# One decoder layer on one core: the down projection's sums of weights split in thirds with rooms of their own, a fifth room for raw weights, and transfers in pieces

## The chip, the cores and the metric

The kernel runs on one core of a Trainium2 chip. The metric is device time in microseconds (us) of one execution; lower is better. A core has five engines that run side by side, each taking its own instructions strictly in order: TensorE (PE, matrix products), VectorE (DVE), ScalarE (ACT), GpSimd (POOL) and SyncE (SP). SP, ACT and POOL also start DMA transfers between the chip's main memory and the core's on-chip memory. An instruction that waits for a semaphore holds up all that stand behind it on its engine.

## The reference

```python
h = rmsnorm(x, norm_mix_pre[l])
proj = h @ w_in[l]
...
x = x + rmsnorm(mix @ w_out[l], norm_mix_post[l])
h = rmsnorm(x, norm_mlp_pre[l])
u = jnp.square(jax.nn.relu(h @ w_mlp_up[l]))
x = x + rmsnorm(u @ w_mlp_down[l], norm_mlp_post[l])
```

All is float32: 256 rows of x, model width 2048, MLP width 8192. The part left out is a recurrent branch and a windowed attention, merged by gates. The change concerns the last product, `u @ w_mlp_down` (256 x 8192 by 8192 x 2048), called the down projection here.

## The kernel before

**Products in parts.** Every float32 product is made of three products of rounded parts: a matrix is split into a high part (rounded by ScalarE, `whi`, `thi`) and a low part (the rest, subtracted by VectorE, `wlo`, `tlo`), and TensorE adds high x high, high x low and low x high (`product`, L1171).

**The weight stream.** All weights pass through one `Stream`. A chunk of 128 x 2048 is loaded in two halves of 128 x 1024, numbered through the whole kernel; SP loads a half into one of `WRAW` = 4 raw rooms (`wraw`, L86), ScalarE and VectorE split it (`two_parts`, L104 and L105) into one of `WHALF` = 6 rooms for parts. `half()` hands the next half to the caller and runs ahead: six halves split, four more loaded. A raw room comes free when its low part has been made.

**Stages.** The MLP is done in two groups f of 4096 columns of u. In the up stage of a group, 16 pairs p = 0 to 15 of u are made (`a_pair`), each from four halves, and split for use as left operands (`evacuate`, into `uT[p]`). Then come two down passes (n = 0, 1), each for 1024 columns of the result (`down`). The first up stage starts at half 272 and the four down passes at halves 336, 368, 464 and 496; the pair p of a pass uses halves 2p and 2p+1 of it. In the tables below, halves 356 and 357 are pair 10 of the first pass.

**Seven products for eight.** For the pairs in `SEVEN` (0, 1, 3, 4, 6, 7, 9, 10, 12) the 2 x 2 blocks of the product are formed with seven block products instead of eight, at the price of sums: on the left e (in `evacuate`), on the right three sums of weight blocks T1, T3, T4 of 128 x 512 each (`right_sums`, L61 to L64 on VectorE) which are then split too (`split` in `split_sums`, L150 and L151). Such a step takes 21 matmuls of 512 columns; the other pairs (2, 5, 8, 11, 13, 14, 15) take 24. In the steps of `SUMS_FIRST` (0, 3, 6, 9) the products with T1, T3, T4 come first, in the other SEVEN steps last. The split of a step's sums is put off until the SEVEN step before it has been started (`put_off`).

**Sums made early.** For pairs 4, 7 and 10 of each pass (`SUMMED`) the sums are made long before: `sums_ahead`, a generator that goes on by one step with every half that is used, loads the chunk (`early`, POOL), sums it on VectorE, and stores the sums to main memory (`away`). In the pass they are loaded again as three pieces (`second`, L136).

**Rooms.** A pool of 12 units of 16 KB per partition holds h2T (the normed input), the left operands and the `early` chunks. The scheduler orders each engine's instructions by its own model, so the order is told below from the built program.

Of the kernel before, what the change touches and what calls it, by code (L numbers as in the profile page):

```python
# [18 lines left out]
F32 = mybir.dt.float32  # L19
# [6 lines left out]
P = 128  # L26
D = 2048
S = 256
# [10 lines left out]
SEVEN = (0, 1, 3, 4, 6, 7, 9, 10, 12)  # L39
SUMMED = (4, 7, 10)  # L40
SUMS_FIRST = (0, 3, 6, 9)
APART = (6, 7, 9, 10, 12)
PAIRS = 16


# [8 lines left out]
    return parts  # L54


def right_sums(v, a, b, t):

    l, r = slice(0, 512), slice(512, 1024)
    one, two = t[:, 0:1024], t[:, 1024:1536]  # L60
    v.tensor_tensor(one.rearrange("p (a b) -> p a b", a=2), b[:, l].unsqueeze(1).to_broadcast([P, 2, 512]),  # L61
                    a.rearrange("p (a b) -> p a b", a=2), ALU.add)
    v.tensor_tensor(b[:, l], t[:, l], a[:, r], ALU.add)
    v.tensor_tensor(two, b[:, l], b[:, r], ALU.add)  # L64


class Stream:
# [3 lines left out]
    def __init__(self, nc, pool, chunks, room, sums):  # L71
        self.nc, self.pool, self.chunks, self.room, self.sums = nc, pool, chunks, room, sums
        self.raw, self.parts = {}, {}
        self.loaded = self.split = self.at = FIRST
        self.pin = lambda i: i
        self.high = []
        self.summed, self.put_off, self.last_sums, self.now = {}, [], -1, FIRST
        self.side = []

    def load_to(self, n):  # L80
        while self.loaded < min(n, 2 * len(self.chunks)):
            j = self.loaded
            c = slice(j % 2 * 1024, j % 2 * 1024 + 1024)
            t = self.pool.tile([P, 1024], F32, tag="wraw", bufs=WRAW, name=f"wraw{j}")
            summed = j % 2 and self.summed.get(j // 2)
            self.latest = self.nc.sync.dma_start(t, summed[1] if summed else self.chunks[j // 2][:, c])  # L86
            self.raw[j] = t
            self.loaded += 1
# [35 lines left out]
    def split_sums(self, j):  # L124


        self.load_to(j + 2)
        v = self.nc.vector
        a, b = self.raw.pop(j), self.raw.pop(j + 1)
        summed = self.summed.get(j // 2)  # L130
        if summed:
            pieces = []
            for i in range(3):
                c = slice(i * 512, i * 512 + 512)
                pieces.append((c, self.room("second")))
                self.nc.gpsimd.dma_start(pieces[i][1], summed[0][:, c])  # L136
        else:
            t = self.sums_room("t")
            right_sums(v, a, b, t)
            pieces = [(slice(0, 1536), t)]  # L140
        (ahi, alo), (bhi, blo) = self.two_parts(a, j), self.two_parts(b, j + 1)
        l, r = slice(0, 512), slice(512, 1024)
        parts = {"B11": (ahi[:, l], alo[:, l]), "B22": (ahi[:, r], alo[:, r]), "T2": (bhi[:, l], blo[:, l]),
                 "B21": (bhi[:, r], blo[:, r])}
        self.parts[j] = parts

        def split():
            hi, lo = [self.sums_room(n).bitcast(F32R) for n in ("thi", "tlo")]
            for c, t in pieces:
                self.nc.scalar.copy(hi[:, c], t)  # L150
                v.tensor_tensor(lo[:, c], t, hi[:, c].bitcast(F32), ALU.subtract)  # L151
            for i, name in enumerate(("T1", "T3", "T4")):
                c = slice(i * 512, i * 512 + 512)
                parts[name] = hi[:, c], lo[:, c]

        self.put_off.append((self.last_sums, split))
        self.last_sums = j
        self.settle()
# [44 lines left out]
def layer(tc, x, few, kx_first, kx_rest, pos_row, gains, w_q, w_xy, w_rg, w_g, w_rp, w_ap, w_out,  # L203
# [47 lines left out]
    def flat(t):  # L251
        return t.rearrange("p a b c -> p (a b c)")
# [900 lines left out]
    def evacuate(p, u, dst):  # L1153
        nc.vector.scalar_tensor_tensor(wide(u), wide(u), 0.0, r2.unsqueeze(1).to_broadcast([P, 2, S]), ALU.max,
                                       ALU.mult)
        nc.scalar.activation(u, u, AF.Square)
        if p not in SEVEN:
            nc.scalar.copy(dst[:, :, 0, :], wide(u))
            nc.vector.tensor_tensor(dst[:, :, 1, :], wide(u), dst[:, :, 0, :].bitcast(F32), ALU.subtract)
            return  # L1160

        e = u2("e")
        u4, e4 = [t.rearrange("p (a b) -> p a b", a=4) for t in (u, e)]
        nc.vector.tensor_tensor(e4[:, 0:2], u[:, 0:P].unsqueeze(1).to_broadcast([P, 2, P]), u4[:, 1:3], ALU.subtract)
        nc.vector.tensor_tensor(e4[:, 2], e4[:, 1], u4[:, 1], ALU.subtract)
        nc.vector.tensor_tensor(e4[:, 3], e4[:, 2], u4[:, 3], ALU.add)
        for to, of in ((dst[:, :, 0:3], u4[:, 1:4]), (dst[:, :, 3:7], e4)):
            nc.scalar.copy(to[:, 0], of)
            nc.vector.tensor_tensor(to[:, 1], of, to[:, 0].bitcast(F32), ALU.subtract)

    def product(b, a, w, begun, tail=False, shared=False):  # L1171

        for i, (x, y) in enumerate(((0, 0), (0, 1), (1, 0))):
            mm(b, a[x], w[y], start=not begun and i == 0, stop=tail and i == 2, skip_group_check=shared)  # L1174
# [7 lines left out]
    def down(f, n, uT, held, order, finish, early, between=lambda p: None, behind=lambda: None, closing=False):  # L1182
# [20 lines left out]
        for p in range(PAIRS - held - closing):  # L1203
            if p in SEVEN:
                parts = ws.seven()
                names = list(LEFT)
                if p in SUMS_FIRST:
                    names.sort(key=lambda name: LEFT[name][1] not in ("T1", "T3", "T4"))
                else:
                    names.sort(key=lambda name: LEFT[name][1] in ("T1", "T3", "T4"))  # L1210
                for name in names:
                    i, w = LEFT[name]
                    product(banks[name], (uT[p][:, 0, i], uT[p][:, 1, i]), parts[w], name in begun,
                            p == SEVEN[-1] and (name in ("P1", "P6", "Q5", "N7") or closing and name == PLACE[order[-1]]))
                    begun.add(name)
                if p == SEVEN[-1]:
# [47 lines left out]
    for f in range(2):  # L1264
        uT = {}
        rooms = []
        if f:
            ws.side += [sums_ahead(c, 9, 6, lambda: ws.sums_room("t")) for c in summed[9:]]
        full = []
        for p in range(PAIRS):  # L1270
            u = u2("u")
            if f == 0 and p < 2:
                up_pair(p, wide(u))
            else:
                a_pair(h2T, wide(u), PRIO if p == PAIRS - 1 else 0)
            full.append((p, u))
            if f == 0 and p == R2_AT:
                pump(99)
                spread_r2()
                ctx3.close()  # L1280
                pc = ctx2.enter_context(tc.tile_pool(name="pc", bufs=1))
                ws.room = u2
                ws.sums_room = lambda tag: pc.tile([P, 1536], F32, tag=tag, name=tag)
                ws.side += [sums_ahead(c, 7, 4, lambda: ws.sums_room("t")) for c in summed[6:9]]
            if f == 1 or p >= R2_AT:
                for q, u in full:
                    if q in APART:
                        uT[q] = flat(unit(f"seven{f}{q}"))[:, 0 : 14 * P].rearrange("p (a b c) -> p a b c", a=2, b=7)
                    elif q in SEVEN:
                        uT[q] = pc.tile([P, 2, 7, P], F32R, tag="seven", bufs=len(SEVEN) - len(APART),  # L1290
                                        name=f"seven{f}{q}")
                    elif q == PAIRS - 1:
                        uT[q] = pc.tile([P, 2, 2, S], F32R, tag="plain", name=f"plain{f}")
                    else:
                        i = sum(k not in SEVEN for k in range(q))
                        if i % 2 == 0:
                            rooms.append(unit(f"uT{f}{i}"))
                        uT[q] = rooms[i // 2][:, 2 * (i % 2) : 2 * (i % 2) + 2]
# [158 lines left out]
```

## Time and profile before

| | |
|---|---|
| median of 3 runs | 1507.63 us (1503.21 to 1509.97) |
| the profiled execution's own time | 1507.84 us |
| its span in the trace | 1506.1 us |
| TensorE busy | 1485.7 us (99%) |
| VectorE busy | 1132.3 us (75%) |
| ScalarE busy | 843.6 us (56%) |
| GpSimd busy | 40.5 us (3%) |
| main memory read and written | 222 GB/s over the span |

All times in the trace are counted from the span's start. In a row of the timeline stand start, duration, engine, line, operation, out<-in, and in brackets the engine's idle time just before and what ended it. In a row of the groups stand the count, the busy time, the mean duration in ns, and the idle time with what ended it. In the chain of waits stand start, duration and what the end of the run was waiting for then. A line of the page is a line of the kernel above.

### The profile page before, as it was taken

To read this page: it belongs to the slowest core of one execution; us is meant where nothing else is said; L and a number is where in the kernel's file an instruction comes from. 1 tells how busy PE (TensorE), PEld (TensorE's weight loads), DVE (VectorE), ACT (ScalarE), POOL (GpSimd) and SP (SyncE) were. 2 spreads that over 40 slices of the span, in tenths; PEclk is the share of its full clock that TensorE was granted. 3 is DMA by queue.
4 is the path that set the end of the run, shared out by engine and by line. 5 is a ranking of instruction groups with operands and counts; after the bars stand their busy time and mean duration, and the time that the engine had idled before them with its cause. 6 is when DMAs were issued, how large, how long until landed. Compare 5 with 4: busy or idle time off the path is not lost.

```text
span 1506.1 us, 20243 instructions
## 1 busy us (share of the span) xinstructions
PE 1485.7 (99%) x7562; PEld 1254.8 (83%) x7562; DVE 1132.3 (75%) x1439; ACT 843.6 (56%) x1181; POOL 40.5 (3%) x81
## 2 busy tenths in 40 slices
PE   9999999999999999999999999999999999999997
PEld 8887778888889888888889888887778888887776
DVE  6676668759578866666658887787887767689987
ACT  7564565647477674444346655565464555456563
POOL 0000000000000000000000000000000000000000
PEclk9999999999999999999999999999999999999999
DMA  9753544555645659787766676576678666677675
GB/s 338 234 165 134 185 160 139 176 183 188 203 158 193 219 174 343 263 303 249 266 214 234 234 282 224 196 241 219 221 258 301 224 219 227 208 261 240 212 248 189
DMA packets 91971, 336.06 MB, mean 223 GB/s; under 512 B 10465, under 2 KB 10721, under 8 KB 89313
## 3 DMA queue, kind: packets, MB, share of 16 engines
q1 hardware_dynamic: 80352, 288.89, 57.1%
q0 software_dynamic: 8064, 37.75, 6.9%
q10 hardware_dynamic: 3456, 8.13, 1.4%
q8 instruction: 59, 0.97, 0.3%
q14 instruction: 40, 0.32, 0.1%
HBM read 312.71 MB, written 22.02 MB: 222 GB/s over the span
## 4 chain that ended last, share of the span: by engine, by line
PE 74%; DVE 9%; DMA 9%; ACT 4%; issue 3%; DVEq 0%; ACTq 0%; SPq 0%
PE ps L293 21%; PE ps L291 11%; DMA wraw<-in_w_dn 6%; DVE wlo L105 4%; PE pp L335 3%; PE pp L333 3%; PE pp L331 3%; PE g L331 3%; PE g L335 3%; PE g L333 3%; ACT whi L104 2%; PE q L331 2%; PE q L335 2%; PE q L333 2%; PE o L331 2%
## 5 line engine op out<-in xcount | busy, mean ns | idle before, releaser
L104 ACT CAST whi<-wraw 128x1024 fp32r<-128x1024 f32 x516 | 537.4, 1051 | 520.5 <-PE ps L293 103.0
L105 DVE TENSOR_TENSOR wlo<-wraw,whi 128x1024 fp32r<-128x1024 f32 x516 | 623.5, 1220 | 270.4 <-ACT whi L104 266.0
L293 PE MATMUL ps<-h2T,whi 128*128 128x512 f32 x960 | 223.9, 390 | 0.0
L293 PEld LDWEIGHTS ps<-h2T,whi 128*128 128x128 f32 x960 | 178.2, 188 | 35.6
L291 PEld LDWEIGHTS ps<-h2T,wlo 128*128 128x128 f32 x960 | 119.1, 192 | 2.3
L293 PE MATMUL ps<-hT,whi 128*128 128x512 f32 x512 | 120.6, 391 | 0.0
L291 PE MATMUL ps<-h2T,wlo 128*128 128x256 f32 x960 | 119.9, 283 | 0.0
L293 PEld LDWEIGHTS ps<-hT,whi 128*128 128x128 f32 x512 | 94.7, 188 | 19.5 <-issue 0.7
L331 PE MATMUL g<-whi,hT 128*128 128x512 f32 x256 | 101.1, 395 | 0.0
L335 PE MATMUL g<-whi,hT 128*128 128x512 f32 x256 | 99.8, 390 | 0.0
L333 PE MATMUL g<-wlo,hT 128*128 128x512 f32 x256 | 99.7, 390 | 0.0
L1174 PE MATMUL dQ<-whi,uT 128*128 128x512 f32 (+1 forms) x192 | 71.9, 387 | 0.0
L291 PEld LDWEIGHTS ps<-hT,wlo 128*128 128x128 f32 x512 | 63.7, 191 | 2.1 <-issue 0.8
L291 PE MATMUL ps<-hT,wlo 128*128 128x256 f32 x512 | 64.6, 283 | 0.0
L331 PEld LDWEIGHTS g<-whi,hT 128*128 128x128 f32 x256 | 48.1, 188 | 10.5 <-issue 1.0
L335 PEld LDWEIGHTS g<-whi,hT 128*128 128x128 f32 x256 | 48.1, 188 | 10.3
L333 PEld LDWEIGHTS g<-wlo,hT 128*128 128x128 f32 x256 | 48.1, 188 | 9.5
L1174 PE MATMUL s<-whi,seven 128*128 128x512 f32 x144 | 53.5, 389 | 0.0
L331 PE MATMUL q<-whi,hT 128*128 128x512 f32 x128 | 51.1, 400 | 0.0
L1174 PE MATMUL s<-thi,seven 128*128 128x512 f32 x144 | 51.0, 395 | 0.0
L331 PE MATMUL pp<-whi,yrnn 128*128 128x512 f32 x128 | 50.0, 391 | 0.0
L335 PE MATMUL q<-whi,hT 128*128 128x512 f32 x128 | 49.9, 390 | 0.0
(324 smaller groups left out, 2607.5 us busy)
## 6 DMA issues: line engine op xcount, KB each, us to landing
wraw<-in_w_up SPq DMA_DIRECT2D x128, 512.0 KB, 4.4
wraw<-in_w_dn SPq DMA_DIRECT2D x116, 512.0 KB, 4.5
wraw<-in_w_g SPq DMA_DIRECT2D x64, 512.0 KB, 4.4
wraw<-in_w_xy SPq DMA_DIRECT2D x64, 512.0 KB, 4.0
wraw<-in_w_q SPq DMA_DIRECT2D x32, 512.0 KB, 3.7
wraw<-in_w_ap SPq DMA_DIRECT2D x32, 512.0 KB, 3.8
wraw<-in_w_rp SPq DMA_DIRECT2D x32, 512.0 KB, 5.0
wraw<-in_w_out SPq DMA_DIRECT2D x32, 512.0 KB, 4.6
```

The lines of the kernel that those rows point to most:

```text
L104: self.pin(self.nc.scalar.copy(hi, src))
L105: self.pin(self.nc.vector.tensor_tensor(lo, src, hi.bitcast(F32), ALU.subtract))
L291: mm(ps[:, f, 1, :], w, a[:, 0, :], start=False, stop=j == 1 and k == 7)
L293: mm(ps[:, f].rearrange("p a b -> p (a b)"), w, a.rearrange("p a b -> p (a b)"), start=kt == 0, stop=j == 3 and k == 7)
L331: mm(banks[tb][n], a[:, 0, t], hi[:, n * 512 : n * 512 + 512], start=first, stop=False)
L333: mm(banks[tb][n], a[:, 0, t], lo[:, n * 512 : n * 512 + 512], start=False, stop=False)
L335: mm(banks[tb][n], a[:, 1, t], hi[:, n * 512 : n * 512 + 512], start=False, stop=last)
L1174: mm(b, a[x], w[y], start=not begun and i == 0, stop=tail and i == 2, skip_group_check=shared)
```

## The change

The changed kernel does the following:

- **Thirds.** T1, T3 and T4 of a step get a room each for high and low part (`thi` and `tlo`, three rooms of 128 x 512 each, in place of one room each of 128 x 1536). Sums made in the pass are split by three instructions of 512 columns on ScalarE and on VectorE where one of 1536 stood. The sums themselves lie in two rooms (`t1024`, `t512`).
- **Order of products.** In a SEVEN step the products with sums go T1, T3, T4; before, it was T4, T1, T3.
- **A fifth raw room.** From the first up stage on, each half whose number divides by five goes to `xraw`, and the stream loads one half further ahead.
- **Transfers in pieces.** `sums_ahead` loads its chunk in four quarters of 128 x 512, with generator steps between them, and stores sums as 128 x 1024 and 128 x 512, again with steps between. A chunk takes 11 or 16 steps where it took 9, 11 or 15.
- **Left operands.** Two neighbouring pairs share a unit (8 units for 16 pairs); of a SEVEN pair, three of seven blocks lie in a room `three` of their own.

```diff
+    def left(three_four, i):
+        t, k = three_four[i > 2], i if i < 3 else i - 3
+        return t[:, 0, k], t[:, 1, k]
...
+            self.wide = self.wide or self.more and j % (WRAW + 1) == 0
+            t = self.more() if self.wide and j % (WRAW + 1) == 0 else self.pool.tile([P, 1024], F32, tag="wraw", bufs=WRAW, name=f"wraw{j}")
...
-            t = self.sums_room("t")
-            right_sums(v, a, b, t)
-            pieces = [(slice(0, 1536), t)]
+            one, two = self.sums_rooms()
+            right_sums(v, a, b, one, two)
+            pieces = [one[:, 0:512], one[:, 512:1024], two]
...
-            hi, lo = [self.sums_room(n).bitcast(F32R) for n in ("thi", "tlo")]
-            for c, t in pieces:
-                self.nc.scalar.copy(hi[:, c], t)
-                v.tensor_tensor(lo[:, c], t, hi[:, c].bitcast(F32), ALU.subtract)
...
+            for name, t in zip(("T1", "T3", "T4"), pieces):
+                hi, lo = [self.sums_room(n) for n in ("thi", "tlo")]
+                self.nc.scalar.copy(hi, t)
+                v.tensor_tensor(lo, t, hi.bitcast(F32), ALU.subtract)
+                parts[name] = hi, lo
...
-        self.load_to(max(FIRST, j + WHALF) + WRAW)
+        self.load_to(max(FIRST, j + WHALF) + WRAW + bool(self.wide))
...
-    def sums_ahead(c, first, second, room):
+    def sums_ahead(c, gaps, rooms):
         w = flat(unit("early", F32))
-        nc.gpsimd.dma_start(w, chunks[c])
-        for _ in range(first):
+        for i in range(4):
+            nc.gpsimd.dma_start(w[:, quarter(i)], chunks[c][:, quarter(i)])
+            for _ in range(gaps[0]):
+                yield
+        for _ in range(gaps[1]):
             yield
-        t = room()
-        right_sums(nc.vector, w[:, 0:1024], w[:, 1024:2048], t)
-        nc.gpsimd.dma_start(ws.summed[c][0], t)
-        nc.gpsimd.dma_start(ws.summed[c][1], w[:, 1024:2048])
-        for _ in range(second):
-            yield
+        one, two = rooms()
+        right_sums(nc.vector, w[:, 0:1024], w[:, 1024:2048], one, two)
+        to, b = ws.summed[c]
+        for away, of in ((to[:, 0:1024], one), (to[:, 1024:1536], two), (b, w[:, 1024:2048])):
+            nc.gpsimd.dma_start(away, of)
+            for _ in range(gaps[2]):
+                yield
...
-    ws.side += [sums_ahead(c, 5, 4, lambda: flat(unit("early_t", F32))[:, 0:1536]) for c in summed[:6]]
+    ws.side += [sums_ahead(c, (1, 4, 1), unit_rooms) for c in summed[:6]]
...
-            ws.side += [sums_ahead(c, 9, 6, lambda: ws.sums_room("t")) for c in summed[9:]]
+            ws.side += [sums_ahead(c, (2, 5, 1), ws.sums_rooms) for c in summed[9:]]
...
-                ws.sums_room = lambda tag: pc.tile([P, 1536], F32, tag=tag, name=tag)
-                ws.side += [sums_ahead(c, 7, 4, lambda: ws.sums_room("t")) for c in summed[6:9]]
+                ws.more = lambda: pc.tile([P, 1024], F32, tag="xraw", name="xraw")
+                ws.sums_room = lambda tag: pc.tile([P, 512], F32R, tag=tag, bufs=3, name=tag)
+                ws.sums_rooms = lambda: [pc.tile([P, n], F32, tag=f"t{n}", name=f"t{n}") for n in (1024, 512)]
+                ws.side += [sums_ahead(c, (2, 5, 1), ws.sums_rooms) for c in summed[6:9]]
```

What this does to the built order is shown at three places. On VectorE in the first down pass, from the low part of half 357 on, stood before (`t` with `wraw360`, `wraw361`: the sums of pair 12; `tlo` from `t`: pair 9; `tlo` from `second`: pair 10):

```order
L105 TENSOR_TENSOR wlo357_9031<-wraw357_8948,whi357_9030 128x1024
L151 TENSOR_TENSOR tlo_9017<-t_8979,thi_9016 128x1536
L105 TENSOR_TENSOR wlo358_9051<-wraw358_8991,whi358_9050 128x1024
L61 TENSOR_TENSOR t_9103<-wraw361_9036,wraw360_9034 128x1024
L105 TENSOR_TENSOR wlo359_9069<-wraw359_8993,whi359_9068 128x1024
L63 TENSOR_TENSOR wraw361_9036<-t_9103,wraw360_9034 128x512
L151 TENSOR_TENSOR tlo_9096<-second_9020,thi_9095 128x512
L151 TENSOR_TENSOR tlo_9096<-second_9022,thi_9095 128x512
L151 TENSOR_TENSOR tlo_9096<-second_9024,thi_9095 128x512
```

And in the changed kernel stands there:

```order
L105 TENSOR_TENSOR wlo357_9129<-wraw357_9015,whi357_9128 128x1024
L149 TENSOR_TENSOR tlo_9107<-t1024_9068,thi_9106 128x512
L149 TENSOR_TENSOR tlo_9111<-t1024_9068,thi_9110 128x512
L149 TENSOR_TENSOR tlo_9115<-t512_9069,thi_9114 128x512
L59 TENSOR_TENSOR t1024_9205<-wraw361_9132,xraw_9083 128x1024
L105 TENSOR_TENSOR wlo358_9149<-wraw358_9033,whi358_9148 128x1024
L61 TENSOR_TENSOR wraw361_9132<-t1024_9205,xraw_9083 128x512
L62 TENSOR_TENSOR t512_9206<-wraw361_9132 128x512
L105 TENSOR_TENSOR wlo359_9167<-wraw359_9081,whi359_9166 128x1024
L149 TENSOR_TENSOR tlo_9194<-second_9118,thi_9193 128x512
L149 TENSOR_TENSOR tlo_9198<-second_9119,thi_9197 128x512
L149 TENSOR_TENSOR tlo_9202<-second_9120,thi_9201 128x512
```

The first sum of pair 12 moved ahead of the low part of half 358, the last sum ahead of half 359, and pair 9's split became three instructions. Of the 24 places where sums are made in the passes, one had a lower half's low part behind the sums before; now 11 have one or two (pairs 0 and 1 of the first and third pass; pairs 9 and 12 of the first; 0, 9 and 12 of the second; 0 and 12 of the fourth).

On TensorE at the first SEVEN step of the first pass stood (`dQ_8698` is the bank of T4's product, `s_8695` holds those of T1 and T3):

```order
L1174 MATMUL dQ_8698<-thi,seven_7331 128x512
L1174 MATMUL dQ_8698<-tlo,seven_7331 128x512
L1174 MATMUL dQ_8698<-thi,seven_7331 128x512
L1174 MATMUL s_8695<-thi,seven_7331 128x512
L1174 MATMUL s_8695<-tlo,seven_7331 128x512
L1174 MATMUL s_8695<-thi,seven_7331 128x512 x2
```

And now:

```order
L1178 MATMUL s_8750<-thi,uT_7355 128x512
L1178 MATMUL s_8750<-tlo,uT_7355 128x512
L1178 MATMUL s_8750<-thi,uT_7355 128x512 x2
L1178 MATMUL s_8750<-tlo,uT_7355 128x512
L1178 MATMUL s_8750<-thi,uT_7355 128x512
L1178 MATMUL dQ_8753<-thi,three_7356 128x512
```

T4, which is summed last, moved behind T1 and T3.

On POOL's queue in the second down pass (`second<-away_77`: sums of pair 7; `away_79`: of pair 10; `early`: a chunk for the fourth pass) stood:

```order
L136 DMA second<-away_75 128x512 x3
L136 DMA second<-away_77 128x512 x3
L136 DMA second<-away_79 128x512
L361 DMA early<-in_w_dn 128x2048
L136 DMA second<-away_79 128x512 x2
```

And now:

```order
L134 DMA second<-away_75 128x512 x3
L134 DMA second<-away_77 128x512
L358 DMA early<-in_w_dn 128x512 x4
L134 DMA second<-away_77 128x512 x2
L134 DMA second<-away_79 128x512 x3
```

The chunk's load became four, and moved ahead of two of pair 7's pieces. By the program, its unit comes free after pair 1 of that pass; before, it was that of pairs 2 and 5, after pair 5.

More of the change, by code (lines that the diff above doesn't have):

```diff
@@ L78, in __init__ @@
         self.side = []
+        self.more, self.wide = None, False
     def load_to(self, n):
@@ L131, in split_sums @@
         if summed:
[L132 to L136, printed above, removed]
-        else:
-            t = self.sums_room("t")
-            right_sums(v, a, b, t)
-            pieces = [(slice(0, 1536), t)]
+            pieces = [self.room("second") for _ in range(3)]
+            for i, t in enumerate(pieces):
+                self.nc.gpsimd.dma_start(t, summed[0][:, i * 512 : i * 512 + 512])
+        else:
+            one, two = self.sums_rooms()
+            right_sums(v, a, b, one, two)
+            pieces = [one[:, 0:512], one[:, 512:1024], two]
         (ahi, alo), (bhi, blo) = self.two_parts(a, j), self.two_parts(b, j + 1)
@@ L1166, in evacuate @@
         nc.vector.tensor_tensor(e4[:, 3], e4[:, 2], u4[:, 3], ALU.add)
[L1167 removed]
+        for to, of in zip(dst, (u4[:, 1:4], e4)):
             nc.scalar.copy(to[:, 0], of)
@@ L1282, in layer @@
                 ws.room = u2
-                ws.sums_room = lambda tag: pc.tile([P, 1536], F32, tag=tag, name=tag)
-                ws.side += [sums_ahead(c, 7, 4, lambda: ws.sums_room("t")) for c in summed[6:9]]
+                ws.more = lambda: pc.tile([P, 1024], F32, tag="xraw", name="xraw")
+                ws.sums_room = lambda tag: pc.tile([P, 512], F32R, tag=tag, bufs=3, name=tag)
+                ws.sums_rooms = lambda: [pc.tile([P, n], F32, tag=f"t{n}", name=f"t{n}") for n in (1024, 512)]
+                ws.side += [sums_ahead(c, (2, 5, 1), ws.sums_rooms) for c in summed[6:9]]
             if f == 1 or p >= R2_AT:
                 for q, u in full:
[L1287 to L1293, printed above, removed]
-                    else:
[L1295 to L1298, printed above, removed]
+                    if q % 2 == 0:
+                        rooms.append(unit(f"uT{f}{q}"))
+                    room = rooms[-1][:, 2 * (q % 2) : 2 * (q % 2) + 2]
+                    if q in SEVEN:
+                        three = pc.tile([P, 2, 3, P], F32R, tag="three", bufs=len(SEVEN), name=f"three{f}{q}")
+                        uT[q] = three, flat(room).rearrange("p (a b c) -> p a b c", a=2, b=4)
+                    else:
+                        uT[q] = room
                     evacuate(q, u, uT[q])
```

21 lines of the change are left out of this document (8 added, 13 removed).

## The prediction

> **What bounds the kernel now.** I read the page's busy times first, then the windows by stage, then who waited on TensorE.
>
> ```profile
> PE 1485.7 (99%) x7562; PEld 1254.8 (83%) x7562; DVE 1132.3 (75%) x1439; ACT 843.6 (56%) x1181; POOL 40.5 (3%) x81
> 980.00:1066.00 86.00, 83.92 (x362) 68.50 (x361) 72.24 (x74) 46.48 (x50) 3.76 (x7) 0.98 0.68 217
> 1066.00:1152.00 86.00, 81.97 (x357) 66.45 (x356) 67.99 (x70) 44.51 (x48) 6.45 (x12) 1.00 0.81 275
> 1152.00:1323.00 171.00, 171.00 (x982) 151.27 (x981) 124.97 (x154) 94.31 (x117) 3.76 (x7) 1.00 0.67 222
> PE dQ L1174 <- DVE tlo L151: 7.6, 8, 2.1
> PE dQ L1174 <- ACT thi L150: 1.8, 3, 0.9
> ```
>
> TensorE is the bound. In the second up stage (1152 to 1323) it is busy for 171.00 of 171 us: nothing is to be gained there. In the first two down passes it is not (83.92 and 81.97 of 86), and its only long waits are for the split sums, `tlo` and `thi`: 9.4 us in 11 places. That is the part that the change works on.
>
> How much is lost in all comes from start to start, since an end of a matmul is modelled. Rows of the timeline and of the chain of waits:
>
> ```profile
> 980.35 0.39 PE L1174 MATMUL dQ<-thi,seven 128*128 128x512 f32 x1
> 1141.38 2.72 PE dQ L1174 x12
> 1152.26 3.85 PE ps L293 x17
> 1329.91 0.39 PE L1174 MATMUL dQ<-thi,seven 128*128 128x512 f32 x1
> 1493.38 0.28 PE L1174 MATMUL dQ<-whi,uT 128*128 128x256 f32 x1
> 979.00:1153.00 174.00, 165.80 (x714) 134.74 (x714) 0.99 0.74 246
> ```
>
> Twelve matmuls in a row take 2.72 us, 0.2267 each. The first two passes hold 714 (last row): 161.9 us, but last from 980.35 to 1152.26, 171.9 us. **Lost: 10.0 us.** Passes three and four hold 696 of 512 columns up to 1493.38 (714 less the 18 that the kernel makes in halves there): 157.8 us in 163.5. **Lost: 5.7 us.** Together 15.7 us: the most that this change can bring, 1.0% of the time.
>
> The longest loss shows how it comes about. Pair 10 of the first pass, TensorE and then VectorE:
>
> ```profile
> 1033.15 0.39 PE L1174 MATMUL dQ<-thi,seven 128*128 128x512 f32 x1
> 1035.62 0.50 PE L1174 MATMUL dQ<-tlo,seven 128*128 128x512 f32 x1 [2.08 <-DVE tlo L151]
> 1038.51 0.63 PE L1174 MATMUL dQ<-whi,uT 128*128 128x512 f32 x1
> 1016.30 1.89 DVE L151 TENSOR_TENSOR tlo<-second,thi 128x512 fp32r<-128x512 f32 x3
> 1020.44 3.49 DVE L105 TENSOR_TENSOR wlo<-wraw,whi 128x1024 fp32r<-128x1024 f32 x3
> 1023.85 1.75 DVE L151 TENSOR_TENSOR tlo<-t,thi 128x1536 fp32r<-128x1536 f32 x1
> 1025.52 1.22 DVE L105 TENSOR_TENSOR wlo<-wraw,whi 128x1024 fp32r<-128x1024 f32 x1
> 1030.80 1.23 DVE L61 TENSOR_TENSOR t<-wraw,wraw 128x1024 f32<-128x1024 f32 x1 [4.07 <-DMA wraw<-in_w_dn]
> 1033.08 0.68 DVE L63 TENSOR_TENSOR wraw<-t,wraw 128x512 f32<-128x512 f32 x1
> 1033.68 1.89 DVE L151 TENSOR_TENSOR tlo<-second,thi 128x512 fp32r<-128x512 f32 x3
> 1023.96 6.72 DMA wraw<-in_w_dn
> ```
>
> The last `wlo` of the row at 1020.44 (half 357) frees a raw room at 1023.9. The load of half 361 starts into it at 1023.96 and takes 6.72 us. VectorE stands idle for 4.07 us at the sums of pair 12, which need that half; pair 10's `tlo`, whose pieces were ready, stand behind and come at 1033.68. TensorE needs T4, the last piece, at once, and starts at 1035.62. Afterwards its matmuls ran at a lower pace (0.63 long at 1038.51) for about 3 us, which adds some 1.6 us to the 2.2 of the wait.
>
> In the second pass it is pair 3, whose sums are made in the pass:
>
> ```profile
> 1066.25 7.67 DMA wraw<-in_w_dn
> 1076.27 1.24 DVE t L61
> 1079.25 1.48 ACT thi L150
> 1080.77 1.76 DVE L151 TENSOR_TENSOR tlo<-t,thi 128x1536 fp32r<-128x1536 f32 x1 [0.16 <-ACT thi L150]
> 1082.58 0.50 PE L1174 MATMUL dQ<-tlo,seven 128*128 128x512 f32 x1 [1.29 <-DVE tlo L151]
> ```
>
> A load waited for a room, took 7.67 us, then came the sums, one split of 1.48 us, and one of 1.76 us, and only then TensorE. SP's queue of loads in these passes is held by rooms nearly all the time (138 of 172 us):
>
> ```profile
> SPq L86 <- DVE wlo L105: 107.8, 57, 7.2
> SPq L86 <- DVE wraw L63: 30.6, 5, 7.6
> DVE t L61 <- DMA wraw<-in_w_dn: 12.5, 7, 4.1
> ```
>
> **The change part by part.**
>
> *Thirds.* Their cost, from the groups by form:
>
> ```profile
> L151 DVE TENSOR_TENSOR tlo<-t,thi 128x1536 fp32r<-128x1536 f32 x24 | 42.1, 1755 | 2.5 <-ACT thi L150 2.3
> L150 ACT CAST thi<-t 128x1536 fp32r<-128x1536 f32 x24 | 35.4, 1476 | 2.5 <-PE s L1174 1.9 <-DVE t L64 0.6
> L151 DVE TENSOR_TENSOR tlo<-second,thi 128x512 fp32r<-128x512 f32 x36 | 22.6, 684 | 0.0
> L150 ACT CAST thi<-second 128x512 fp32r<-128x512 f32 x36 | 19.9, 616 | 2.9 <-PE s L1174 2.9
> ```
>
> 24 times one instruction becomes three. On VectorE three in a row took 1.89 us (row at 1016.30) against 1.755: 24 x 0.135 = 3.2 us; apart, 3 x 0.684 - 1.755 = 0.297, in all 7.1 us. On ScalarE at most 24 x 0.372 = 8.9 us. I take 3.2, since the order has most of them in a row. VectorE works 72.24 and 67.99 of 86 us in a pass, so 0.8 to 1.8 us a pass fit into its idle time; if that cover were gone, 3.2 to 7.1 us would lie on the path. [...]
>
> What thirds bring: for sums made in the pass, the first product needs 0.62 + 0.68 = 1.30 us of splitting in place of 1.48 + 1.76 = 3.24, 1.9 us sooner; each further third takes 0.68, as long as its three matmuls. For loaded sums, with T1 first, one of three pieces is needed in place of three: 1.89 - 0.68 = 1.2 us sooner. And each third's room comes free for the next step while TensorE still uses the others.
>
> *Fifth room.* A load starts at the low part of the half before: at least one `wlo` sooner (3.49 / 3 = 1.16 us), at most one half of TensorE's work (161.9 us over 64 halves, 2.5 us). Traffic stays the same.
>
> *Order on VectorE.* The scheduler spent part of that room: 11 places have sums ahead of lower halves. At pair 10's place `tlo` now stands behind one more sum of 512 columns, about 0.6 us by the spacing of rows 1033.08 and 1033.68; half 358 stands behind the wait for 361. Per loss, then: sooner by 1.2 + 1.2 - 0.6 = 1.8 us at least and 1.9 + 2.5 = 4.4 at most.
>
> *Pieces.* Twelve chunks, each 3 loads and 1 store more: 48 issues on POOL. From the DMA issues of the first passes and the groups:
>
> ```profile
> early<-in_w_dn POOLq DMA_DIRECT2D x2, 1024.0 KB, 9.0
> second<-away POOLq DMA_DIRECT2D x15, 256.0 KB, 6.2
> L136 POOL DMA_DIRECT2D second<-away x36 | 19.4, 539 | 359.9 <-DVE tlo L151 106.9 <-DVE seven L1169 87.8 <-ACT t L1343 47.0
> ```
>
> 48 x 0.54 = 26 us on an engine that is busy 3%: no cost. The last quarter is loaded 5 or 7 halves before its sum; at 2.72 us a half that is 13.6 or 19 us, over the 9.0 of the whole chunk. Without that cover, VectorE would wait up to 9.0 us in each of twelve places. On POOL's queue in the second pass, the load that now stands ahead of pair 7's pieces waits for pair 1; pair 7's sums are used 28 us later (two plain steps at 5.44, three SEVEN at 4.76, and 12 matmuls), over 9.0 + 6.2. I cost this at nothing. Left operands: the same instructions, at nothing.
>
> *Sum.* The credit of 1.8 to 4.4 us covers most of the 11 waits (the longest idle 2.1 us), but the largest only in part at its lower end, and in the third pass loads of other things share the DMA engines. I leave 4.4 of the 15.7 us: 11.3 recovered, 1507.84 - 11.3 = **1496.5 us**. The profiled execution lies 0.2 us from the median of the runs shown, so the forecast holds for either. Its own range: 1492.1 (all recovered) to 1500.
>
> **The rivals.**
>
> *The order spends the room.* VectorE waits for half 361 as before, only one instruction earlier. For it: the 11 places. Against: the load starts sooner there too. Then only the thirds count, 1.2 us less 0.6 in each of 11 places: 6.6 us, and the time is 1501. Chance 0.16.
>
> *VectorE becomes the bound.* If the idle time in the passes turns out to be no cover, the split costs 3.2 to 7.1 us and the losses stay: 1511 to 1515. Against: 14 and 18 us idle a pass. [...] Chance 0.06.
>
> *The fifth load brings nothing.* If DMA engines limit the loads (share 0.81, 275 GB/s in the second pass), a fifth in flight makes each slower, and it goes as in the first rival or to 1506. Against: 0.68 and 217 GB/s in the first pass, which loses as much. [...] Chance 0.06.
>
> *Slower: near halves stand behind far loads.* In seven places inside the passes (pairs 9 and 12; 0, 9, 12; 0, 12) the low part of a half that TensorE uses earlier waits for a load that it does not need. If VectorE has no lead there, each costs the wait of 4.07 us and a `wlo` of 1.16: 7 x 5.2 = 37 us, 1533 with the gain taken off, 1515 if it is half. It decides from (7.5 + 11.3) / 7 = 2.7 us a place. Against: in the trace half 358 was split by 1026.7 (row at 1025.52) and used at 1038.51, a lead of 12 us. Chance 0.12.
>
> **How the numbers follow.** The forecast has 0.60, the rivals 0.16, 0.06, 0.06 and 0.12. About 0.5%, 7.5 us, is what a measurement of this kernel can tell from no change. Faster by over that (under about 1500) is the forecast: 0.60. Within it lie the first three rivals: 0.28. Slower: 0.12. The range from 1491.5 to 1507 takes in forecast, first rival and part of the third.
>
> **What would show it.** Right: TensorE's waits for `tlo` and `thi` from 9.4 us to under 4, the sums' wait for loads (12.5 us) smaller, first two passes under 167 us, up stages still at 171 of 171. Wrong: waits of TensorE for `wlo`, or new ones before 980 us; SP's wait for rooms unchanged; matmuls longer than 0.39 in more places.

## The result, and the profile after

The changed kernel takes 1497.45 us (median of 6 runs, 1496.26 to 1499.64) where the kernel before took 1505.54 us beside it (6 runs). The ratio is 0.9946, with a 95% interval of 0.9928 to 0.9963: faster by 0.54% (0.37 to 0.72), about the half per cent that can be told from no change. The forecast was 1496.5 us. The profiled execution has a span of 1494.5 us against 1506.1 before, 11.6 us less, and it is this difference that is taken apart below. It is larger than the 8.1 us between the medians, since the profiled execution before took 1507.84 us, 2.3 over its median, and that of the changed kernel 1496.26, 1.2 under its own; these 3.5 us are spread from execution to execution and are not explained here.

The changed kernel's busy times and its windows of the first two down passes and the second up stage; after the duration come busy time and count for TensorE, its weight loads, VectorE, ScalarE and GpSimd, then granted clock, DMA share and GB/s:

```profile
PE 1481.0 (99%) x7562; PEld 1255.3 (84%) x7562; DVE 1133.2 (76%) x1487; ACT 850.9 (57%) x1229; POOL 66.7 (4%) x129
980.00:1066.00 86.00, 86.00 (x387) 71.47 (x386) 76.38 (x91) 51.21 (x67) 4.41 (x9) 1.00 0.70 232
1066.00:1152.00 86.00, 86.00 (x386) 71.43 (x385) 73.16 (x85) 49.91 (x62) 10.14 (x19) 1.00 0.83 289
1152.00:1323.00 171.00, 171.00 (x991) 151.64 (x990) 125.95 (x158) 92.65 (x118) 6.69 (x13) 1.00 0.65 217
```

TensorE is now busy for all of the down passes' windows. From the first to the last matmul of the first two passes, and of passes three and four (timeline of the changed kernel):

```profile
984.88 0.39 PE L1178 MATMUL s<-thi,uT 128*128 128x512 f32 x1
1146.50 0.39 PE L1178 MATMUL dCs<-whi,uT 128*128 128x512 f32 x1
1324.54 0.39 PE L1178 MATMUL s<-thi,uT 128*128 128x512 f32 x1
1486.49 0.28 PE L1178 MATMUL s<-whi,uT 128*128 128x256 f32 x1
```

The first row gives the start of the first of 714 matmuls and the second that of the last, so 161.62 us hold 713 steps of 0.2267: nothing is lost. Measured so in every trace, the kernel before has 171.5 and 167.7 us, the changed one 161.6 and 161.95. So 15.6 of the 15.7 us that the prediction named have gone, where it had expected 11.3.

But the first pass begins at 984.88 us, 4.5 us later than before. All waits of TensorE of over 0.5 us in the changed kernel, with total, times and longest:

```profile
PE o L329 <- DVE wlo L105: 2.9, 1, 2.9
PE warm L433 <- DVE ones L417: 1.1, 1, 1.1
PE kv L455 <- ACT hT L439: 0.8, 1, 0.8
PE o L327 <- ACT whi L104: 0.7, 1, 0.7
```

No wait for `tlo` or `thi` is left. A new one has come, for `wlo` in the projection of the mixer's output (L327 and L329, "o"). TensorE, VectorE and POOL there (the timeline, one engine after the other; in a POOL row L358 is the load of a quarter, L367 a store of sums):

```profile
743.04 0.39 PE L331 MATMUL o<-whi,mixT 128*128 128x512 f32 x1
744.14 0.49 PE L327 MATMUL o<-whi,mixT 128*128 128x512 f32 x1 [0.71 <-ACT whi L104]
747.53 0.50 PE L329 MATMUL o<-wlo,mixT 128*128 128x512 f32 x1 [2.90 <-DVE wlo L105]
752.68 0.40 PE L327 MATMUL o<-whi,mixT 128*128 128x512 f32 x1
...
726.58 4.90 DVE L954 TENSOR_TENSOR xg<-x,g 128x512 f32<-128x512 f32 x8
731.39 1.22 DVE L59 TENSOR_TENSOR early_t<-early 128x1024 f32<-128x1024 f32 x1
745.11 1.23 DVE L59 TENSOR_TENSOR early_t<-early 128x1024 f32<-128x1024 f32 x1 [2.95 <-DMA early<-in_w_dn]
746.26 2.35 DVE L105 TENSOR_TENSOR wlo<-wraw,whi 128x1024 fp32r<-128x1024 f32 x2
...
703.32 1.09 POOL L358 DMA_DIRECT2D early<-in_w_dn  x2 [44.90 <-PE pp L331]
733.02 0.54 POOL L367 DMA_DIRECT2D away<-early_t  x1 [28.62 <-DVE early_t L59]
736.50 0.54 POOL L367 DMA_DIRECT2D away<-early_t  x1 [1.19 <-DVE early_t L62]
737.07 1.11 POOL L358 DMA_DIRECT2D early<-in_w_dn  x2
```

Read from below. POOL issues two quarters of the sixth chunk at 703. Next in its queue stand the three stores of the fifth chunk, and POOL waits 28.62 us for the sums that they carry, which VectorE begins at 731.39, after its work for the norm. Only at 737.07 do the last two quarters of the sixth chunk go. VectorE comes to the sums of that chunk and waits 2.95 us for its third quarter, and the low parts that TensorE needs stand behind. From 743.04 to 752.68 there are 16 steps from matmul to matmul, 3.6 us at 0.2267 each; they took 9.6. So 6.0 us are lost there. The bill of the span: 15.6 us less in the down passes, 6.0 more here, 1.5 less elsewhere before them, 0.5 less at the end: 11.6.

### The profile page after: what moved, and what is told of

Read it like the earlier page. It is cut to its first block, busy times and chain, and to the rows that moved or that the text cites. A ratio compares the mean times of both kernels' runs of the same rounds, so it can differ in the third digit from the quotient of the medians.

```text
span 1494.5 us, 20497 instructions
## 1 busy us (share of the span) xinstructions
PE 1481.0 (99%) x7562; PEld 1255.3 (84%) x7562; DVE 1133.2 (76%) x1487; ACT 850.9 (57%) x1229; POOL 66.7 (4%) x129
## 4 chain that ended last, share of the span: by engine, by line
PE 95%; DVE 2%; DMA 2%; ACT 1%; issue 0%; DVEq 0%; SPq 0%; ACTq 0%
PE ps L289 21%; PE ps L287 11%; PE dQ L1178 8%; PE s L1178 7%; PE dP L1178 4%; PE g L327 4%; PE g L331 4%; PE g L329 4%; PE pp L331 4%; PE pp L327 4%; PE pp L329 4%; PE dCs L1178 3%; PE q L327 2%; PE q L331 2%; PE q L329 2%; PE kv L455 1%
## 5 line engine op out<-in xcount | busy, mean ns | idle before, releaser
L105 DVE TENSOR_TENSOR wlo<-wraw,whi 128x1024 fp32r<-128x1024 f32 x469 | 567.8, 1221 | 245.9 <-ACT whi L104 242.5
L104 ACT CAST whi<-wraw 128x1024 fp32r<-128x1024 f32 x469 | 490.4, 1051 | 439.2 <-PE ps L289 94.2
L1178 PE MATMUL dQ<-whi,uT 128*128 128x512 f32 (+1 forms) x296 | 108.7, 385 | 0.0
L327 PE MATMUL g<-whi,hT 128*128 128x512 f32 x256 | 101.1, 395 | 0.0
L329 PE MATMUL g<-wlo,hT 128*128 128x512 f32 x256 | 99.7, 390 | 0.0
L104 ACT CAST whi<-xraw 128x1024 fp32r<-128x1024 f32 x47 | 49.4, 1052 | 45.6 <-PE ps L289 21.9
L105 DVE TENSOR_TENSOR wlo<-xraw,whi 128x1024 fp32r<-128x1024 f32 x47 | 57.4, 1221 | 14.9 <-ACT whi L104 14.9
L1178 PEld LDWEIGHTS dQ<-whi,uT 128*128 128x128 f32 x296 | 55.2, 188 | 11.2
L148 ACT CAST thi<-t 128x512 fp32r<-128x512 f32 x72 | 41.6, 617 | 31.2 <-PE s L1178 20.0
L327 PEld LDWEIGHTS g<-whi,hT 128*128 128x128 f32 x256 | 48.1, 188 | 10.6 <-issue 1.0
L1178 PE MATMUL dQ<-wlo,uT 128*128 128x512 f32 (+1 forms) x148 | 56.9, 385 | 0.0
L358 POOL DMA_DIRECT2D early<-in_w_dn x48 | 26.1, 543 | 690.1 <-DVE px L317 497.6
```

The costliest lines, as they stand in the source:

```text
L104: self.pin(self.nc.scalar.copy(hi, src))
L105: self.pin(self.nc.vector.tensor_tensor(lo, src, hi.bitcast(F32), ALU.subtract))
L148: self.nc.scalar.copy(hi, t)
L327: mm(banks[tb][n], a[:, 0, t], hi[:, n * 512 : n * 512 + 512], start=first, stop=False)
L329: mm(banks[tb][n], a[:, 0, t], lo[:, n * 512 : n * 512 + 512], start=False, stop=False)
L358: nc.gpsimd.dma_start(w[:, quarter(i)], chunks[c][:, quarter(i)])
```

## The experiments

Two questions were open: whether the loss near 743 us comes from the quarters themselves or from where they stand, and which part of the change filled the down passes. "Lost" is the time of the four down passes, measured as above, over the 323.56 us of the changed kernel. Every ratio is to the kernel before, run beside it; its medians were 1505.5 to 1505.9 us.

**The wait near 743 us.** First run: whole chunks, with the 9, 11 and 15 steps of before (the diff shows the load alone).

```diff
-        for i in range(4):
-            nc.gpsimd.dma_start(w[:, quarter(i)], chunks[c][:, quarter(i)])
...
+        nc.gpsimd.dma_start(w, chunks[c])
```

> The changed kernel with each chunk that is summed ahead loaded in one transfer again, sums 5, 7 or 9 halves later and the three stores in a row, as before the change. Theory (quarters spaced out made the sixth chunk's sums late, and they hold up wlo in the o-projection; in the down passes the quarters do nothing): TensorE's waits for wlo and whi near 743 us (3.6 us, and some 1.5 us of slower matmuls behind them) go, the four down passes stay without a gap, so 1492 to 1493.5 us against 1497.5 of the changed kernel. Rival (whole chunks of 1 MB crowd the loads of the down passes, so the quarters are what filled them): up to 15.7 us of gaps come back there, 1497 to 1505 us.

1493.37 us, ratio 0.9921 (0.9902 to 0.9940). The wait for `wlo` has gone, and 1.0 us is lost in the down passes. So the quarters did not fill those: the rival falls. Since the steps changed with the quarters, this run doesn't tell which of them made the wait.

Second run: the quarters stay, and a chunk takes 7 steps in place of 11.

```diff
-    ws.side += [sums_ahead(c, (1, 4, 1), unit_rooms) for c in summed[:6]]
+    ws.side += [sums_ahead(c, (1, 3, 0), unit_rooms) for c in summed[:6]]
```

> The changed kernel with gaps of (1, 3, 0) in place of (1, 4, 1) for the first six chunks: quarters as in the changed kernel, but 7 halves from chunk to chunk in place of 11, and the three stores in a row. All six are then summed ahead of the o-projection's loads on VectorE. Theory (only the lateness of the sixth chunk costs): the waits near 743 us go, 1492 to 1493.5 us. Rival 1 (the quarters' issues or their spread themselves disturb the stage before 980 us): a wait of some 3 to 5 us remains somewhere between 570 and 980 us, 1496 to 1498 us. Rival 2 (the cover of 3 + 1 halves is too short): VectorE waits for early at several of six places and TensorE with it, over 1498 us.

1492.52 us, ratio 0.9919 (0.9901 to 0.9937); 0.4 us lost in the down passes. Quarters as such cost nothing: what cost was that the sixth chunk came late. To separate this from chance, the changed kernel, this one and one with 8 steps were run together.

> The changed kernel itself once more, on the same chip as the three beside it, so that the 4.6 us at 743 us are read off in the same runs. Theory: 1496 to 1498.5 us, some 4 to 5 us over the run with gaps of (1, 3, 0), with TensorE's wait for wlo at 743 us in its trace. Rival (that wait was chance of one profile): no such wait, and the same time as with (1, 3, 0).

> Gaps of (1, 3, 0) for the first six chunks once more, on the same chip as the changed kernel. Theory: 1491.5 to 1493.5 us. Rival: within 1 us of the changed kernel.

```diff
-    ws.side += [sums_ahead(c, (1, 4, 1), unit_rooms) for c in summed[:6]]
+    ws.side += [sums_ahead(c, (1, 4, 0), unit_rooms) for c in summed[:6]]
```

> Gaps of (1, 4, 0): 8 halves from chunk to chunk, six chunks still summed ahead of the o-projection's loads. Theory (any spacing that has the sixth chunk done by then is as good, the last quarter's cover does not matter): within 1 us of the run with (1, 3, 0). Rival (a longer cover takes away the wait of 1.3 us at 602 us): 1.3 us less.

The changed kernel: 1497.44 us, 0.9946 (0.9933 to 0.9958). Gaps of (1, 3, 0): 1492.24 us, 0.9916 (0.9903 to 0.9930). Gaps of (1, 4, 0): 1492.86 us, 0.9922 (0.9908 to 0.9936). The first two intervals lie apart: 5.2 us. TensorE's longest wait after the first 10 us in the trace of the changed kernel, and in that of (1, 3, 0):

```profile
PE o L329 <- DVE wlo L105: 2.8, 1, 2.8
```

```profile
PE ptr L893 <- DVE g L911: 0.8, 1, 0.8
```

The wait at 743 us is there in each readable trace with 11 steps a chunk, and in none with 7, 8 or 9; the wait for `g`, near 602 us, has gone with 8 as well, but that doesn't show in the medians. Gaps of (1, 3, 0) give a version that beats both kernels; those of (1, 4, 0) are as good within the intervals, so one step of cover more or less makes no difference that can be measured. Gaps of (1, 4, 0) leave out only the steps between the stores of the changed kernel, three for each chunk, and in its trace the wait is gone: these steps brought it.

**The down passes.** Each of the two kinds of rooms was taken away alone, first from the changed kernel.

```diff
-                ws.more = lambda: pc.tile([P, 1024], F32, tag="xraw", name="xraw")
```

> The changed kernel without the fifth room for raw halves: four rooms and one load less in flight, all else as changed. Theory (loads start too late for lack of a room, thirds alone win only 1.2 to 1.9 us less 0.6 in each of 11 places): 5 to 9 of the 15.7 us come back in the down passes, 1502 to 1507 us. Rival (thirds alone do it: splitting and freeing by thirds was what held the sums): the down passes stay without gaps, 1497 to 1498 us.

1499.17 us, 0.9959 (0.9945 to 0.9972). Neither theory's number: only 2.6 us are lost in the down passes, where 5 to 9 had been expected. The rest is the same loss near 743 us.

```diff
-                ws.sums_room = lambda tag: pc.tile([P, 512], F32R, tag=tag, bufs=3, name=tag)
+                ws.sums_room = lambda tag: pc.tile([P, 1536], F32R, tag=tag, name=tag)
...
-            for name, t in zip(("T1", "T3", "T4"), pieces):
-                hi, lo = [self.sums_room(n) for n in ("thi", "tlo")]
+            hi, lo = [self.sums_room(n) for n in ("thi", "tlo")]
+            for c, t in pieces:
```

> The changed kernel with one room of 1536 columns each for the sums and their high and low parts again (sums made in the pass split by one instruction of 1536 columns, and the next split waits until all three products have used the room); fifth room, order of products and quarters as changed. VectorE's work falls by 3 to 7 us in all. Theory (thirds and fifth room each bring a part): 3 to 8 us come back in the down passes, mostly where sums are made in the pass (pair 3 of the second), 1500 to 1505 us. Rival (the fifth room alone does it): no gaps, 1497 to 1498 us, or less with VectorE's work.

1500.30 us, 0.9958 (0.9944 to 0.9972). In the range of the theory, but the loss near 743 us is in it as well, so this alone does not tell the two apart. Its one trace spans 3018 us, twice the others, and says nothing of the waits.

So the four corners were run without that loss, with gaps of (1, 3, 0). Edits as in the two diffs, alone and together:

> The kernel with gaps of (1, 3, 0) for the first six chunks (1492.5 us, no gap in the down passes), with one room of 1536 columns each for sums, high and low parts again: fifth room and new order alone. Without the fifth room but with thirds, the trace showed only 1.3 us of gaps in the down passes. Theory (the two overlap: each alone makes TensorE's operands early enough by about 2 us, so either covers most places): 2 to 4 us of gaps, 1494 to 1497 us. Rival (thirds carry it, the fifth room little): 7 us or more, over 1499 us.

> Gaps of (1, 3, 0), thirds as changed, no fifth room: the fourth corner beside both (1492.5), fifth room alone (1494.6) and neither (1503.75). Theory (the two overlap; without the fifth room the down passes lost 1.1 + 1.4 us in the earlier trace): 1494 to 1496 us. Rival (without the fifth room it loses more once the wait at 743 us is gone, since loads then start elsewhere): over 1497 us.

> The kernel with gaps of (1, 3, 0), with neither the fifth room nor thirds: what is left of the change is the order of products (T1, T3, T4), the rooms of the left operands, and the quarters. Theory (thirds and fifth room overlap, and without both the losses are back, save about 1.2 us at each of the places where loaded sums are used first): 7 to 13 us of gaps in the down passes, 1500 to 1505 us. Rival (the order of products is what did it, and the two rooms are not needed): under 3 us of gaps, 1493 to 1496 us.

| with gaps of (1, 3, 0) | median, us | ratio (95% interval) | lost in the down passes |
|---|---|---|---|
| neither | 1503.75 | 0.9991 (0.9981 to 1.0000) | 10.0 us |
| fifth room alone | 1494.64 | 0.9924 (0.9912 to 0.9937) | 1.3 us |
| thirds alone | 1495.77 | 0.9936 (0.9924 to 0.9949) | 3.1 us |
| both, two sets of runs | 1492.24, 1492.52 | 0.9916, 0.9919 | 0.8 us, 0.4 us |

The theory holds in the times, though the fifth room alone lost 1.3 us where 2 to 4 had been expected: alone the fifth room is worth 9.1 us and thirds 8.0, together 11.2 to 11.5. Not all of these ran side by side; by the ratios it is 10.1, 8.3 and 10.8 to 11.3. They overlap. That both are faster than one alone is not shown by the times, whose intervals overlap; the losses in the traces say so (0.4 and 0.8 us against 1.3 and 3.1). How they overlap is seen at pair 3 of the second pass, where the prediction had seen the sums come too late. In each fence the first sum of the pair, the split of the first third (of the whole in the first two), and TensorE's first product that needs it; neither, fifth room alone, thirds alone, and the changed kernel with both:

```profile
1073.67 1.23 DVE L59 TENSOR_TENSOR t<-wraw,wraw 128x1024 f32<-128x1024 f32 x1 [0.50 <-DMA wraw<-in_w_dn]
1078.17 1.76 DVE L150 TENSOR_TENSOR tlo<-t,thi 128x1536 fp32r<-128x1536 f32 x1 [0.15 <-ACT thi L149]
1079.99 0.50 PE L1181 MATMUL s<-tlo,uT 128*128 128x512 f32 x1 [1.29 <-DVE tlo L150]
```

```profile
1072.04 1.22 DVE L59 TENSOR_TENSOR t<-xraw,wraw 128x1024 f32<-128x1024 f32 x1
1076.53 1.76 DVE L150 TENSOR_TENSOR tlo<-t,thi 128x1536 fp32r<-128x1536 f32 x1
1079.73 0.39 PE L1181 MATMUL s<-tlo,uT 128*128 128x512 f32 x1
```

```profile
1071.04 1.22 DVE L59 TENSOR_TENSOR t<-wraw,wraw 128x1024 f32<-128x1024 f32 x1 [2.59 <-issue]
1073.92 0.68 DVE L149 TENSOR_TENSOR tlo<-t,thi 128x512 fp32r<-128x512 f32 x1
1077.31 0.39 PE L1178 MATMUL s<-tlo,uT 128*128 128x512 f32 x1
```

```profile
1072.05 1.22 DVE L59 TENSOR_TENSOR t<-xraw,wraw 128x1024 f32<-128x1024 f32 x1
1074.92 0.69 DVE L149 TENSOR_TENSOR tlo<-t,thi 128x512 fp32r<-128x512 f32 x1
1080.99 0.39 PE L1178 MATMUL s<-tlo,uT 128*128 128x512 f32 x1
```

TensorE stands idle for 1.3 us with neither; from the end of the split to the product that needs it there are 1.4 us in hand with the fifth room, 2.7 with thirds, 5.4 with both. The two traces of both rooms with gaps of (1, 3, 0) have 5.4 and 4.7 there. So at this place the leads add up (gains of 2.7, 4.0, and 6.7 for both), within the 0.7 us by which two traces of one kernel differ; the losses do not, since a lead beyond zero buys nothing.

The order of the products was put back by itself, with both rooms and with neither.

```diff
-                names.sort(key=lambda name: ("T1", "T3", "T4").index(LEFT[name][1]) if LEFT[name][1] in ("T1", "T3", "T4")
-                           else 9 if p in SUMS_FIRST else -1)
+                if p in SUMS_FIRST:
+                    names.sort(key=lambda name: LEFT[name][1] not in ("T1", "T3", "T4"))
+                else:
+                    names.sort(key=lambda name: LEFT[name][1] in ("T1", "T3", "T4"))
```

> The kernel with gaps of (1, 3, 0), thirds and fifth room as changed, but the products in the order of before (T4, T1, T3): TensorE's first product waits for the last third. Theory (the order is worth 1.3 us sooner, and the fifth room alone covers that): within 1 us, 1492 to 1494 us. Rival (the order is the larger part of the gain): 4 us or more of gaps at the pairs where sums come first, over 1496 us.

> As the run with neither, and with the products in the order of before (T4, T1, T3) as well: of the change only the rooms of the left operands and the quarters with gaps of (1, 3, 0) are left. Theory (these do nothing for the down passes): the losses of before, 12 to 16 us, 1503 to 1507 us. Rival (the quarters fill VectorE's waits for the loads that crowd with whole chunks, or the left operands' rooms free VectorE): under 8 us of gaps, under 1500 us.

With both rooms: 1494.40 us, 0.9925 (0.9913 to 0.9937), 4.1 us lost, most of them at one place. That is neither account's number: the loss is the rival's, the time lies between the two. With neither: 1504.62 us, 0.9994 (0.9985 to 1.0002), 12.6 us lost, as the theory had it. The waits for the sums' parts of the first, then of the second:

```profile
PE dQ L1178 <- DVE tlo L149: 2.8, 2, 2.5
```

```profile
PE dQ L1181 <- DVE tlo L150: 6.4, 8, 1.4
PE dQ L1181 <- ACT thi L149: 1.7, 3, 0.9
```

The traces give the order 2.6 us with neither room and 3.2 to 3.6 with both, the medians 0.9 and 1.9 to 2.2; the intervals overlap in both cases. That the order brings something is likely, and its size stays open. The other parts, quarters and left operands with gaps of (1, 3, 0), make no difference that can be measured (0.9994).

## Why the prediction was right or wrong

**What bounds it: right.** The loss was where it was read, by start to start, and of the size that was read: 15.7 us named, 15.6 gone. The up stage stayed at 171.00 of 171, and the sums' wait for loads in the first two passes fell from 12.5 to 10.0 us, as the signs said.

**The credit of a place: too small, the first mis-sized term.** The prediction gave each loss 1.8 to 4.4 us and left 4.4 of 15.7 standing. At pair 3 of the second pass the lead grew by 6.7 us. Of this, from the rows above: the first sum begins 2.7 us sooner against TensorE's need with the fifth room (forecast 1.16 to 2.5), 1.2 us sooner with thirds alone (the prediction named rooms that come free sooner but gave them no size; whether that is the cause is not shown, since the trace names nothing for the 2.59 us that VectorE waits before that sum), and from the first sum to the first split third it takes 3.6 in place of 6.3 us (forecast 1.9 of gain, measured 2.7).

**"The order spends the room": it came, and cost nothing.** At pair 10 of the first pass VectorE still stands before the sums that need half 361, in the changed kernel:

```profile
1031.00 1.23 DVE L59 TENSOR_TENSOR t<-wraw,xraw 128x1024 f32<-128x1024 f32 x1 [3.76 <-DMA wraw<-in_w_dn]
1035.74 1.28 DVE L149 TENSOR_TENSOR tlo<-second,thi 128x512 fp32r<-128x512 f32 x2
1037.47 0.39 PE L1178 MATMUL s<-tlo,uT 128*128 128x512 f32 x1
```

It idles 3.76 us where it idled 4.07, and pair 10's split stands behind it, as the rival said. But measured from the start of the pass the sum begins at 46.1 us in place of 50.5, and the first third is ready about 1 us before TensorE asks.

**Thirds' cost: right.** The splits of sums made in the pass, on VectorE in the changed kernel:

```profile
L149 DVE TENSOR_TENSOR tlo<-t,thi 128x512 fp32r<-128x512 f32 x72 | 46.5, 686 | 1.2 <-ACT thi L148 1.2
```

They cover 46.5 us where it was 42.1: 4.4 us more, between the 3.2 that was taken and the 7.1 of single instructions. VectorE's whole busy time rose by 0.9 us only (1132.3 to 1133.2), and it works 76.4 and 73.2 of 86 us in a pass; ScalarE's rose by 7.3 (843.6 to 850.9), under the bound of 8.9. The rival in which VectorE becomes the bound falls. The sum of the single durations rose by 7.3 (72 of 0.686, 49.4 us, against 42.1); as neighbours overlap in the trace (46.5 us covered by those 49.4), the time covered rose by less.

**"Pieces cost nothing": wrong, the step that failed.** The issues themselves were sized right: GpSimd's busy time rose by 26.2 us, at no cost. The cover was counted in halves from the issue to the sum: 13.6 us. It took for granted that the last quarters are issued when the generator comes to them. In four of the first six chunks (the second, third, fifth and sixth) they stood behind stores of the chunk before, which waited for VectorE. Only at the sixth did VectorE then wait: its third quarter was issued at 737.07, wanted at 742.2 (745.11 less 2.95), and landed at 745.0. The prediction had named the price ("VectorE would wait up to 9.0 us") and the sign ("new ones before 980 us"), but had looked at POOL's queue in the second pass alone. It counted 48 issues and not 11 steps in place of 9: two halves more for each chunk, ten by the start of the sixth, and that pushed its sums into the projection.

**"The fifth load brings nothing": wrong,** it is worth 9.1 us without thirds; with thirds it is 3.3 to 3.5, which the intervals don't tell from nothing. Loads of `early` in the changed kernel, in the down stages and from 560 to 980 us, and the same two with whole chunks (the first run above):

```profile
early<-in_w_dn POOLq DMA_DIRECT2D x12, 256.0 KB, 8.7
early<-in_w_dn POOLq DMA_DIRECT2D x32, 256.0 KB, 6.6
```

```profile
early<-in_w_dn POOLq DMA_DIRECT2D x3, 1024.0 KB, 8.7
early<-in_w_dn POOLq DMA_DIRECT2D x8, 1024.0 KB, 9.4
```

In the down stages the four quarters of a chunk were issued one behind the other, within 2.2 us, so these 8.7 us are not those of a quarter alone. From the first issue to the last landing the three chunks took 7.9, 12.8 and 11.8 us there, and 7.3, 9.3 and 8.7 whole. Yet the time is the same with either (1492.5 and 1493.4), since nobody waits for it where there is cover.

**"Near halves behind far loads": did not come.** TensorE has no wait for `wlo` in the passes of the changed kernel.

**A sign that was badly chosen.** "SP's wait for rooms unchanged" was to speak against the forecast. First two passes, changed kernel:

```profile
SPq L86 <- DVE wlo L105: 126.9, 64, 8.5
SPq L86 <- DVE wraw L61: 14.0, 3, 4.9
SPq L86 <- DVE xraw L61: 4.3, 1, 4.3
```

145 us where it was 138, with nothing lost. Here a queue that runs one load further ahead waits for rooms just as long; only who needs the load can tell.

The forecast of 1496.5 against 1497.45 us was thus right in its mechanism for the passes and in its sign. That it came so close is luck: 4.3 us more were recovered in the passes, 6.0 us were lost in a place that was costed at nothing, and the 1507.84 us that the 11.3 were taken from lie 2.3 over the median of the kernel before, which is 8.1 us above the changed one.

## What to carry to other kernels

A place waits or it doesn't: add up leads (they did add up at the one place that was measured), compare them with zero, and don't add up the savings of two edits that shorten the same chain. When a transfer is cut up or spread out, ask what stands ahead of its last piece on the queue that issues it and what that waits for, and count how far the whole sequence is pushed back: here 11 steps in place of 7 cost 5.2 of the 13.2 us that the best version wins. When a cover is given in steps of work, test it at every place where the steps fall into another stage.

## What the hardware showed unexpectedly

A pause of TensorE can cost more than itself, and its length alone does not decide. Windows around four pauses, with the granted clock in the third column from the end: the kernel before at 1035, the changed one at 748, the fifth room alone at 647, and both rooms with the old order at 1114:

```profile
1033.00:1035.60 2.60, 0.54 (x3) 0.12 (x1) 2.60 (x6) 1.76 (x2) 0.00 (x0) 1.00 0.55 186
1037.00:1038.50 1.50, 1.50 (x5) 1.14 (x4) 1.50 (x3) 0.37 (x1) 0.00 (x0) 0.50 0.09 22
```

```profile
743.00:748.00 5.00, 1.39 (x5) 0.61 (x5) 2.89 (x3) 3.14 (x3) 0.54 (x1) 1.00 0.81 324
748.00:752.00 4.00, 3.94 (x12) 2.73 (x11) 4.00 (x5) 1.05 (x1) 1.09 (x2) 0.57 0.94 290
```

```profile
647.00:649.30 2.30, 0.33 (x3) 0.11 (x2) 2.30 (x5) 0.81 (x2) 1.07 (x2) 1.00 0.82 299
650.80:652.50 1.70, 1.70 (x5) 1.31 (x5) 1.70 (x3) 1.16 (x2) 0.00 (x0) 0.50 0.78 296
```

```profile
1114.00:1117.00 3.00, 0.52 (x4) 0.10 (x2) 3.00 (x5) 2.33 (x3) 0.00 (x0) 1.00 0.66 233
1117.00:1118.50 1.50, 1.50 (x7) 1.22 (x8) 1.50 (x2) 0.70 (x2) 0.00 (x0) 1.00 0.58 199
```

Pauses of 2.47, 3.39 and 2.36 us from start to start were followed by a stretch at half clock (0.43 from matmul to matmul); one of 2.87 us was not: the clock stays at 1.00 in the row behind it. (The 2.36 us are the 1.97 us without a matmul in the row from 647.00 and the 0.39 of one matmul.) The granted clock on record in the traces of the two kernels gives the times more closely. In both, the stretch at half clock ahead of the end lasts 3.413 us (from 1036.45 and from 748.25 us), and the stretches at full clock on either side of it are multiples of that to within 0.03: 302.03 and 135.01 of them in the kernel before, 218.02 and 216.02 in the changed one. Laid on this grid, the pauses of 2.47 and 3.39 us have 2.47 and 2.69 us within one window of 3.413 us, and the window behind it is the slow one. Add up the pauses over 0.5 us in each window of these two traces, from 10 us to the end of the last pass: the two windows ahead of a slow one have 2.47 and 2.83 us (0.14 of it from a shorter pause), and every other one has 2.02 us or less. Where the pause of 2.87 us lies against such windows, and why no slow stretch came behind it, is not shown. One more thing stays open: in the changed kernel's second trace the granted clock is 0.996 over the span, where the first has 0.997, behind a wait of about the same length (2.8 and 2.9 us). Of the 6.0 us near 743 us, 3.6 are waits; most of the rest lies in this stretch, where eight steps from 748.11 to 751.75 us took 3.64 us in place of 1.81.
